# Layer norms between the stages of a two-layer decoder trunk: one GpSimd operation instead of four, residuals of the next weights behind the first modulated chunks, the accumulator filled later

## The chip, the core and the metric

The kernel runs on one core of one Trainium2 chip. The time is what the device measures for one execution, in microseconds (us). The kernel before has a median of 2310.28 us over three runs (2306.4, 2310.28 and 2311.95).

## The reference, cut to what matters

Two layers; each has a token mixer (forgetting attention in layer 0, sliding-window attention in layer 1) and then a gated ConvFFN. SEQ is 256, D_MODEL 2048, everything is float32.

```python
def layer_norm(x, g, b):
    mu = jnp.mean(xf, axis=-1, keepdims=True)
    var = jnp.mean(jnp.square(xf - mu), axis=-1, keepdims=True)
    y = (xf - mu) * lax.rsqrt(var + LN_EPS)
    return (y * g + b)
# every sub-layer:
# x <- LayerNorm(alpha * x + (1 + gate) * F(x * (1 + scale) + shift))
# shift, scale, gate: one vector of 2048 each, from the conditioning c times ada_w, plus ada_b
```

## The kernel before, in words

**Weights.** A float32 product is made of three reduced-precision ones. Each weight tile of 512 KB comes in by a DMA on the SP queue; ACT casts it to `wh` (L258); DVE takes the residual `wl = w - wh` (L269); PE multiplies the activations' halves `hH` and `hL` with `wh`, and `hH` with `wl`. There are four `wh`/`wl` buffers of each kind. `stream` makes one closure per tile, `go`, and puts it in the list `work`; `settle` calls the closures in turn, and `rest` emits the residuals of the tiles that stand next in `work`, across stage borders too: closures that are no tile (those added with `then`) are skipped and do not count.

**Borders.** Four sub-layers run one after the other, so there are three borders between stages and one end. Border 1 lies between layer 0's attention and its ConvFFN (about 492 to 507 us in the trace), border 2 between that and layer 1's attention (1258 to 1272), border 3 between layer 1's attention and its ConvFFN (1535 to 1555). At a border `residual` handles the last 512 columns for t = 0 and t = 1 (two halves of 128 rows each, called t0 and t1 below): DVE multiplies by the gate (L559, tile `t`), adds to `x` (L561), takes the statistics (L563, `stats`) and aggregates them (L566, `mv`: mean and variance). Then POOL (GpSimd) adds EPS (L568) and raises to -0.5 (L569), which gives `rs`; for t0 it also makes -mean * rs in two operations (L571, L572). `normalise` applies them 512 columns at a time: t0 on ACT (L582, from `rs` and the product), t1 on DVE (L584, from mean and `rs`). `between` calls `release` (below), `merged` (L616 to L618, vectors `G` and `B` on DVE) and `modulate`, which makes 8 chunks of two 128-column blocks each: PE transposes (L461), ACT writes `hH` (L471), DVE writes `t` and `hL` (L472, L473). Two chunks are made at once; the other six wait in the list `feeds`, and one follows each weight tile.

**The vectors from ada_w.** In the background `ada_vector` makes ten more vectors of shift, scale or gate: 32 tiles `wa` each, one DVE operation per tile into the accumulator `acc` (L384). `ada_tick` runs such a step whenever a rate that differs by stage has added up to one; `ada_need(l, v)` runs all steps still missing for a vector at the moment when it is wanted. At the end of a vector PE sums the partitions: 16 products with one column each (`sums`) and one small DVE operation for the result `cv` (L408). For the vectors in `HELD`, (0,4) and (1,4), which `between` needs at borders 1 and 3, the sums are put off to `release`. The vectors that follow them, (0,5) and (1,5), are gates, made with `row`: POOL clears `acc` first (L373, 128x2048) and a DMA on POOL's queue adds `ada_b` (L374). There is one buffer `acc`, so the clearing waits for the sums of the vector before.

Of the kernel before, what the change touches and what calls it, by code (L numbers as in the profile page):

```python
# [14 lines left out]
ALU = mybir.AluOpType  # L15
# [3 lines left out]
D = 2048  # L19
# [22 lines left out]
def hybrid_trunk(ctx: ExitStack, tc: tile.TileContext, a: dict, out: bass.AP):  # L42
# [34 lines left out]
    def pin(ins, on=True):  # L77

        if on:
            tc.keep_in_program_order(ins)  # L80
# [125 lines left out]

    feeds, post, work = [], [], []

    def then(fn):

        work.append(fn)
        if len(work) == 1 and not ahead[0]:
            settle()
# [9 lines left out]
    def rest(*items):  # L223

        n = 0
        for f in items:
            if f in residuals:
                residuals[f]()
                n += 1
            elif f in weights:  # L230
                n += 1
            if n > 2 - (items[0] not in weights):
                return

    residuals, weights = {}, set()

    def defer(gen):

# [11 lines left out]
    def stream(wsrc, row0, col, ks, use):  # L250

        for kc in ks[::2]:
            r0 = (row0 + kc) * P
            w = wtile()
            pin(nc.sync.dma_start(w, wsrc[r0:r0 + 2 * P, col:col + WB].rearrange("(k p) f -> p k f", p=P)), False)
            h = hl.tile([P, 2, WB], F32R, tag="wh", name="wh")
            l = hl.tile([P, 2, WB], F32R, tag="wl", name="wl")
            pin(nc.scalar.copy(h, w), False)  # L258

            def go(kc=kc, h=h, l=l):  # L260
                ahead[0] -= 1
                run_post()
                use(kc, h, l)
                if feeds:
                    feeds.pop(0)()
                tick()

            def residual_(w=w, h=h, l=l, go=go):
                pin(nc.vector.tensor_tensor(l, w, f32(h), op=ALU.subtract), False)  # L269
                del residuals[go]  # L270

            ahead[0] += 1
            weights.add(go)
            residuals[go] = residual_
            work.append(go)
            settle(2)
# [85 lines left out]
    def ada_vector(l, v):  # L362
        row = v % 3 == 2
        if (l, v) in HELD and HELD[l, v]:
            q = [cst.tile([P, 512], F32, tag=f"ha{i}", name="ha") for i in range(4)]
            part = lambda c, n: q[c // 512][:, c % 512:c % 512 + n]
            step_ = 512
        else:
            acc = cst.tile([P, D], F32, tag="acc", name="acc")
            part = lambda c, n: acc[:, c:c + n]  # L370
            step_ = D // 2
        if row:
            pin(nc.gpsimd.memset(acc, 0.0), True)  # L373
            nc.gpsimd.dma_start(acc[0:1, :], a["ada_b"][l:l + 1, v * D:(v + 1) * D])  # L374
        for k in range(KC):
            for c in range(0, D, D // 2):
                w = wtile("wa").rearrange("p a f -> p (a f)")
                pin(nc.sync.dma_start(w, a["ada_w"][l, k * P:(k + 1) * P, v * D + c:v * D + c + D // 2]), False)
                for o in range(0, D // 2, step_):
                    ac, wo = part(c + o, step_), w[:, o:o + step_]  # L380
                    if k == 0 and not row:
                        pin(nc.vector.tensor_scalar_mul(ac, wo, cact[:, 0:1]), True)
                    else:
                        pin(nc.vector.scalar_tensor_tensor(ac, wo, cact[:, k:k + 1], ac,  # L384
                                                           op0=ALU.mult, op1=ALU.add), True)
                yield
        if row:
            while not ada["gate_free"]:
                yield
            ada["gate_free"] = False  # L390
            g = cst.tile([P, D], F32, tag="gate", name="gate")
            for j in range(D // 512):
                ps = bank()
                mm(ps, ones, acc[:, j * 512:(j + 1) * 512], start=True, stop=True)
                yield
                nc.scalar.activation(g[:, j * 512:(j + 1) * 512], ps, AF.Copy, bias=1.0)
            gates[l, v] = g
            return
        ps = []

        def sums():
            ps.append(bank())
            for k in range(KC):
                pin(mm(ps[0][:, k:k + 1], part(k * P, P), ones[:, 0:1], start=True, stop=True))

        def finish():
            cv = cst.tile([P, KC], F32, tag=f"cv{v}", name="cv")
            pin(nc.vector.scalar_tensor_tensor(cv, ps[0][:, :KC], 1.0 if v % 3 else 0.0,  # L408
                                               acol[:, l, v * KC:(v + 1) * KC], op0=ALU.add, op1=ALU.add), True)
            cols[l, v] = cv  # L410

        if (l, v) in HELD:
            held.append((sums, finish))
            ada["held"] = not HELD[l, v]
            ready_cols.add((l, v))
        else:
            sums()
            yield
            finish()
# [136 lines left out]
    def residual(ps, d, gate, last):  # L556
        for t in range(NT):
            tmp = ttile()
            nc.vector.tensor_tensor(tmp, ps[t], gate[:, d * 512:(d + 1) * 512], op=ALU.mult)  # L559
            xs = x[:, t, d * 512:(d + 1) * 512]  # L560
            nc.vector.tensor_tensor(xs, xs, tmp, op=ALU.add)  # L561
            if last:
                nc.vector.bn_stats(stats[:, t, d, :], xs)  # L563
                if d == D // 512 - 1:
                    mv = sp.tile([P, 2], F32, tag="mv", name="mv")
                    nc.vector.bn_aggr(mv, stats[:, t].rearrange("p a b -> p (a b)"))  # L566
                    rs = sp.tile([P, 2], F32, tag="rs", name="rs")
                    nc.gpsimd.tensor_scalar_add(rs[:, 0:1], mv[:, 1:2], EPS)  # L568
                    nc.gpsimd.tensor_tensor(rs[:, 0:1], rs[:, 0:1], mhalf, op=ALU.pow)  # L569
                    if t == 0:  # L570
                        nc.gpsimd.tensor_tensor(rs[:, 1:2], rs[:, 0:1], mv[:, 0:1], op=ALU.mult)  # L571
                        nc.gpsimd.tensor_scalar_mul(rs[:, 1:2], rs[:, 1:2], -1.0)  # L572
                    moments[t] = (mv[:, 0:1], rs[:, 0:1], rs[:, 1:2])
            yield

# [96 lines left out]
    def out_proj(oT, full, w_o, l):  # L672
        def stat(kc, t):
            while kc not in full:
                step()
            return oT[kc][0][:, t * P:(t + 1) * P], oT[kc][1][:, t * P:(t + 1) * P]

        ps = {d: x_banks() for d in range(2)}

        def part(d, ks):  # L680
            use = x_mm_end(ps[d], stat, KC, 2) if d == D // WB - 1 else                 lambda kc, h, l_: x_mm(ps[d], kc, h, l_, stat, KC - 1)
            stream(w_o, 0, d * WB, ks, use)

        for i, ks in enumerate((range(0, 8), range(8, 12))):
            then(lambda i=i: ada.update(rate=((1.4,1.4,1.8,1.8), (0.9,)*4)[l][i]))
            for d in range(2):
                part(d, list(ks))
        then(lambda: ada_need(l, 2))
        for d in range(D // WB):
            if d < 2:  # L690
                part(d, list(range(12, KC)))
            else:
                then(lambda d=d: ada.update(rate=((1.4,1.4,1.8,1.8), (0.9,)*4)[l][d]))
                ps[d] = x_banks()
                part(d, list(range(KC)))
            then(lambda d=d: defer(residual(ps[d], d, gates[l, 2], True)))
        then(lambda: (flush(), ada.update(gate_free=True)))


    def fox(l, j):  # L700
# [277 lines left out]
    def conv_ffn(l):  # L978
# [37 lines left out]
        for si, (b0, b1) in enumerate(sbs):  # L1016
# [20 lines left out]
            then(ready)  # L1037
            for d in range(D // WB):
                ps = x_stationary(w_dn, d * WB, b0 * 4, (b1 - b0) * 4, stat, (2, 4)[l] if si > 0 and d == D // WB - 1 else 0)
                then(lambda ps=ps, d=d, si=si: defer(residual(ps, d, gates[l, 5], si == len(sbs) - 1)))  # L1040
        then(lambda: (flush(), ada.update(gate_free=True)))


    def between(l, v, g, b, name, ll):

        ada_need(l, v)
        ada_need(l, v + 1)
        release()
        modulate(*merged(l, v, g, b, ll), normalise)
        later([affine(name, ll)])  # L1050

    for l in range(DEPTH):
        if l > 0:
            then(lambda l=l: (between(l, 0, 2, 3, "ln_ffn", l - 1), ada.update(rate=.3)))
            swa(l, l // 2)
        else:
            fox(l, l // 2)
        then(lambda l=l: between(l, 3, 0, 1, "ln_mix", l))
        conv_ffn(l)
    settle()  # L1060
    gb, bb = ln_rows("ln_ffn", DEPTH - 1)
# [34 lines left out]
```

## Time and profile before

| what | value |
|---|---|
| median of the three runs | 2310.28 us (2306.4 to 2311.95) |
| the profiled execution's own time | 2307.69 us |
| its span in the trace | 2305.9 us |
| PE busy (matmul) | 2232.5 us, 97% of the span |
| PE weight load busy | 2047.7 us, 89% |
| DVE busy | 1803.7 us, 78% |
| ACT busy | 1137.8 us, 49% |
| POOL busy | 40.1 us, 2% |
| mean granted TensorE clock | 0.986 of full speed |

The span is the part of the execution that the profiler sees on the core; 1.8 us lie around it. PE is busy nearly all the time, so time can be lost or won where PE waits. POOL is hardly used; what matters there is who waits for it. In the timelines below "start us, us" is the start of a row and how long it ran, `x4` says that four like instructions stand in one row, and the bracket at the end gives the engine's idle time before the row and what ended it.

### The profile page before, as it was taken

How to read it: one execution, taken by the hardware profiler on the slowest of the kernel's cores; microseconds unless marked ns; L12 is line 12 of the kernel's file. 1: busy time of each engine (PE TensorE's matmuls, PEld its weight loads, DVE VectorE, ACT ScalarE, POOL GpSimd, SP SyncE). 2: the span in 40 equal slices, each digit the busy share in tenths (PEclk: the TensorE clock that was granted, in tenths of full speed). 3: DMA queues.
4: the chain of work that ended last, by engine and by line, in shares of the span. 5: the costliest groups of instructions: out<-in, count | busy, mean ns of one | idle time of the engine just before them, and what ended most of it. 6: DMA issues, size and time to landing. Idle time of an engine off the chain costs nothing.

```text
span 2305.9 us, 38661 instructions
## 1 busy us (share of the span) xinstructions
PE 2232.5 (97%) x15061; PEld 2047.7 (89%) x15061; DVE 1803.7 (78%) x2609; ACT 1137.8 (49%) x1685; POOL 40.1 (2%) x79
## 2 busy tenths in 40 slices
PE   5899999899999999999999999999999999999997
PEld 5799988789999988999987778779999988999986
DVE  7888978979977876887886998899878655666656
ACT  1336653545555533454543578745555533455532
POOL 1001000010000000000001000000000000000000
PEclk9999999999999999999999999999999999999999
DMA  9998989969887897887887685788888566666663
GB/s 322 329 351 269 350 321 352 327 212 312 302 263 243 291 312 257 292 285 257 274 299 255 212 302 182 236 291 276 265 265 256 180 193 193 191 188 188 190 191 112
DMA packets 285561, 598.86 MB, mean 260 GB/s; under 512 B 20790, under 2 KB 53816, under 8 KB 285376
## 3 DMA queue, kind: packets, MB, share of 16 engines
q1 hardware_dynamic: 284768, 595.85, 78.4%
q8 instruction: 118, 1.93, 0.3%
q0 software_dynamic: 608, 0.53, 0.1%
q14 instruction: 67, 0.55, 0.1%
HBM read 594.21 MB, written 2.10 MB: 259 GB/s over the span
## 4 chain that ended last, share of the span: by engine, by line
PE 87%; DVE 8%; ACT 3%; issue 2%; POOL 0%; DMA 0%; SPq 0%; DVEq 0%; ACTq 0%; POOLq 0%
PE ws L75 51%; PE xs L75 31%; DVE wl L269 2%; DVE acc L384 2%; PE sm L75 1%; PE cps L75 1%; ACT wh L258 1%; PE S L75 1%; PE o L75 1%; DVE oacc L516 1%; PE sm L461 1%; ACT pr L635 0%; ACT pr L643 0%; PE T L655 0%; DVE x L561 0%
## 5 line engine op out<-in xcount | busy, mean ns | idle before, releaser
L269 DVE TENSOR_TENSOR wl<-w,wh 128x1024 fp32r<-128x1024 f32 x728 | 888.9, 1222 | 397.2 <-ACT wh L258 369.8
L258 ACT CAST wh<-w 128x1024 fp32r<-128x1024 f32 x728 | 764.2, 1052 | 861.5 <-PE ws L75 320.0
L75 PE MATMUL ws<-hH,wh 128*128 128x256 f32 x3328 | 938.9, 282 | 6.0 <-ACT wh L258 6.0
L75 PE MATMUL ws<-hH,wl 128*128 128x256 f32 x3328 | 930.6, 281 | 4.0 <-DVE wl L269 3.9
L75 PE MATMUL ws<-hL,wh 128*128 128x256 f32 x3328 | 931.6, 280 | 0.2 <-DVE hL L85 0.2
L75 PEld LDWEIGHTS ws<-hH,wh 128*128 128x128 f32 x3328 | 629.4, 189 | 10.0 <-ACT wh L258 6.8
L75 PEld LDWEIGHTS ws<-hH,wl 128*128 128x128 f32 x3328 | 627.7, 189 | 5.6 <-DVE wl L269 5.5
L75 PEld LDWEIGHTS ws<-hL,wh 128*128 128x128 f32 x3328 | 629.2, 189 | 2.7 <-issue 1.9
L75 PE MATMUL xs<-wh,gT 128*128 128x512 f32 x1408 | 438.1, 392 | 0.0
L384 DVE SCALAR_TENSOR_TENSOR acc<-wa,cact,acc 128x1024 f32<-128x1024 f32 x308 | 391.8, 1278 | 0.0
L75 PEld LDWEIGHTS xs<-wh,gT 128*128 128x128 f32 x1408 | 266.5, 189 | 55.9
L75 PE MATMUL xs<-wl,gT 128*128 128x512 f32 x704 | 275.7, 392 | 0.0
L75 PEld LDWEIGHTS xs<-wl,gT 128*128 128x128 f32 x704 | 133.3, 189 | 27.3
L75 PE MATMUL xs<-wl,hH 128*128 128x512 f32 x352 | 141.0, 401 | 5.1 <-DVE wl L269 5.1
L75 PE MATMUL xs<-wh,hL 128*128 128x512 f32 x352 | 139.9, 399 | 0.4 <-DVE hL L85 0.4
L75 PE MATMUL xs<-wh,hH 128*128 128x512 f32 x352 | 139.6, 406 | 0.2 <-ACT hH L471 0.2
L75 PE MATMUL xs<-wh,oT 128*128 128x512 f32 x384 | 125.5, 397 | 1.0 <-ACT pT L657 0.9
L985 ACT ACTIVATE u<-ws,ccol 128x256 f32<-128x256 f32 x176 | 96.7, 562 | 58.5 <-PE ws L75 51.3
L986 DVE SCALAR_TENSOR_TENSOR u<-ws,ccol,u 128x255 f32<-128x255 f32 x176 | 82.5, 478 | 20.0 <-ACT u L985 20.0
L75 PEld LDWEIGHTS xs<-wh,oT 128*128 128x128 f32 x384 | 72.6, 190 | 16.1 <-ACT pT L657 1.3
L75 PEld LDWEIGHTS xs<-wl,hH 128*128 128x128 f32 x352 | 66.5, 189 | 22.1 <-DVE wl L269 8.0
L988 DVE SCALAR_TENSOR_TENSOR u<-ws,ccol,u 128x254 f32<-128x254 f32 x176 | 83.4, 478 | 2.0
(211 smaller groups left out, 1559.6 us busy)
## 6 DMA issues: line engine op xcount, KB each, us to landing
w<-in_ffn_w_up_dram SPq DMA_DIRECT2D x352, 512.0 KB, 4.6
wa<-in_ada_w_dram SPq DMA_DIRECT2D x320, 512.0 KB, 5.2
w<-in_ffn_w_down_dram SPq DMA_DIRECT2D x176, 512.0 KB, 5.0
w<-in_fox_w_in_dram SPq DMA_DIRECT2D x96, 512.0 KB, 5.9
wo<-in_ada_w_dram SPq DMA_DIRECT2D x64, 512.0 KB, 7.7
w<-in_swa_w_in_dram SPq DMA_DIRECT2D x40, 512.0 KB, 4.7
w<-in_fox_w_o_dram SPq DMA_DIRECT2D x32, 512.0 KB, 6.8
w<-in_swa_w_o_dram SPq DMA_DIRECT2D x32, 512.0 KB, 5.7
```

Source lines behind the costliest of these rows:

```text
L75: return nc.tensor.matmul(o, lhsT, rhs, start=start, stop=stop, **kw)
L258: pin(nc.scalar.copy(h, w), False)
L269: pin(nc.vector.tensor_tensor(l, w, f32(h), op=ALU.subtract), False)
L384: pin(nc.vector.scalar_tensor_tensor(ac, wo, cact[:, k:k + 1], ac, op0=ALU.mult, op1=ALU.add), True)
L461: nc.tensor.transpose(o[:, t * P:(t + 1) * P], x[:, t, (k + j) * P:(k + j + 1) * P], ident)
L516: nc.vector.scalar_tensor_tensor(acc[:, v, k % 2, :], w[:, k, :], cact[:, kc:kc + 1], acc[:, v, k % 2, :], op0=ALU.mult, op1=ALU.add)
L985: nc.scalar.activation(u, pf, AF.Identity, bias=cw(CW, f), scale=cw(2, f))
L986: nc.vector.scalar_tensor_tensor(u[:, 1:], pf[:, :S - 1], cw(1, f), u[:, 1:], op0=ALU.mult, op1=ALU.add)
L988: nc.vector.scalar_tensor_tensor(u[:, 2:], pf[:, :S - 2], cw(0, f), u[:, 2:], op0=ALU.mult, op1=ALU.add)
```

## The change

It has three parts. (1) In the layer norm EPS is added on DVE, onto the variance in `mv` (new L577); POOL keeps only the power (new L578); for t0 the product -mean * rs is made by one DVE operation (new L580). (2) `rest` stops at a closure that is marked `alone`: the closures at the borders are marked, and while the first two chunks are made no residual of the second and later tiles of the next stage is emitted; the two that come next are pinned behind them (`behind`). (3) A gate vector that follows a held one, (0,5) or (1,5), runs four empty steps before it clears `acc`.

```diff
+    def then(fn, alone=False):
+        if alone:
+            lone.add(fn)
...
         for f in items:
+            if f in lone:
+                n = max(n, 2)
             if f in residuals:
                 residuals[f]()
                 n += 1
...
             def residual_(w=w, h=h, l=l, go=go):
-                pin(nc.vector.tensor_tensor(l, w, f32(h), op=ALU.subtract), False)
+                pin(nc.vector.tensor_tensor(l, w, f32(h), op=ALU.subtract), behind[0] > 0)
+                behind[0] -= 1
                 del residuals[go]
...
         if row:
+            if (l, v - 1) in HELD:
+
+                for _ in range(4):
+                    yield
             pin(nc.gpsimd.memset(acc, 0.0), True)
...
-                    nc.gpsimd.tensor_scalar_add(rs[:, 0:1], mv[:, 1:2], EPS)
-                    nc.gpsimd.tensor_tensor(rs[:, 0:1], rs[:, 0:1], mhalf, op=ALU.pow)
+                    nc.vector.tensor_scalar_add(mv[:, 1:2], mv[:, 1:2], EPS)
+                    nc.gpsimd.tensor_tensor(rs[:, 0:1], mv[:, 1:2], mhalf, op=ALU.pow)
                     if t == 0:
-                        nc.gpsimd.tensor_tensor(rs[:, 1:2], rs[:, 0:1], mv[:, 0:1], op=ALU.mult)
-                        nc.gpsimd.tensor_scalar_mul(rs[:, 1:2], rs[:, 1:2], -1.0)
+                        nc.vector.scalar_tensor_tensor(rs[:, 1:2], mv[:, 0:1], -1.0, rs[:, 0:1],
+                                                       op0=ALU.mult, op1=ALU.mult)
...
-            then(lambda d=d: defer(residual(ps[d], d, gates[l, 2], True)))
-        then(lambda: (flush(), ada.update(gate_free=True)))
+            then(lambda d=d: defer(residual(ps[d], d, gates[l, 2], True)), d == D // WB - 1)
+        then(lambda: (flush(), ada.update(gate_free=True)), True)
...
         modulate(*merged(l, v, g, b, ll), normalise)
+        behind[0] = 2
         later([affine(name, ll)])
```

The last `residual` of layer 1's ConvFFN passes and the calls of `between` get the same mark. Lines of the new kernel have new numbers: L269 is L273 there, L384 is L393, L408 L417, L472 and L473 L481 and L482, L559 to L566 are L568 to L575, L584 L593, L616 to L618 L625 to L627, and the clearing L373 is L382.

How instructions move on DVE at border 1, before, from the aggregation of t0 to the first normalised columns of t1 (`wl` is the residual of a tile of the next stage, `cv` the result of the held vector (0,4)):

```order
L566 BN_AGGR mv<-stats 128x2
L269 TENSOR_TENSOR wl<-w,wh 128x1024
L559 TENSOR_TENSOR t<-xs,gate 128x512
L269 TENSOR_TENSOR wl<-w,wh 128x1024
L561 TENSOR_TENSOR x<-x,t 128x512
L563 BN_STATS stats<-x 128x6
L566 BN_AGGR mv<-stats 128x2
L408 SCALAR_TENSOR_TENSOR cv<-sm,acol 128x16
L616 TENSOR_TENSOR G<-cv,lcol 128x16
L617 TENSOR_TENSOR B<-cv,lcol 128x16
L584 TENSOR_SCALAR x<-x,mv,rs 128x512
```

and the same stretch of DVE in the new kernel:

```order
L575 BN_AGGR mv<-stats 128x2
L577 TENSOR_SCALAR mv<-mv 128x1
L580 SCALAR_TENSOR_TENSOR rs<-mv,rs 128x1
L568 TENSOR_TENSOR t<-xs,gate 128x512
L570 TENSOR_TENSOR x<-x,t 128x512
L572 BN_STATS stats<-x 128x6
L575 BN_AGGR mv<-stats 128x2
L577 TENSOR_SCALAR mv<-mv 128x1
L417 SCALAR_TENSOR_TENSOR cv<-sm,acol 128x16
L593 TENSOR_SCALAR x<-x,mv,rs 128x512
L625 TENSOR_TENSOR G<-cv,lcol 128x16
L626 TENSOR_TENSOR B<-cv,lcol 128x16
```

The two residuals between t0 and t1 are gone (a third, further up, too; they stand behind the two chunks now), t0's product L580 stands between t0 and t1, and G and B stand behind the first normalised columns.

POOL's operations around borders 1 and 2, before (the first clearing is that of gate (0,5), the second that of a later gate):

```order
L568 TENSOR_SCALAR rs<-mv 128x1
L569 TENSOR_TENSOR rs<-rs,mhalf 128x1
L571 TENSOR_TENSOR rs<-rs,mv 128x1
L572 TENSOR_SCALAR rs<-rs 128x1
L568 TENSOR_SCALAR rs<-mv 128x1
L569 TENSOR_TENSOR rs<-rs,mhalf 128x1
L373 MEMSET acc 128x2048
L374 DMA acc<-in_ada_b_dram 1x16x128
```

and in the new kernel, from the powers of border 1 to those of border 2:

```order
L578 TENSOR_TENSOR rs<-mv,mhalf 128x1 x2
L382 MEMSET acc 128x2048
L383 DMA acc<-in_ada_b_dram 1x16x128
L382 MEMSET acc 128x2048
L383 DMA acc<-in_ada_b_dram 1x16x128
L578 TENSOR_TENSOR rs<-mv,mhalf 128x1 x2
```

Three operations for t0 and one for t1 have left POOL; the clearing still stands directly behind the power of t1, and what it waits for is the same last product of the sums as before.

DVE at border 3, before (`acc` rows are steps of the held vector (1,4)), from the last of its steps to the aggregation of t0:

```order
L384 SCALAR_TENSOR_TENSOR acc<-wa,cact,acc 128x1024 x2
L269 TENSOR_TENSOR wl<-w,wh 128x1024 x2
L384 SCALAR_TENSOR_TENSOR acc<-wa,cact,acc 128x1024
L269 TENSOR_TENSOR wl<-w,wh 128x1024 x3
L559 TENSOR_TENSOR t<-xs,gate 128x512
L561 TENSOR_TENSOR x<-x,t 128x512
L563 BN_STATS stats<-x 128x6
L269 TENSOR_TENSOR wl<-w,wh 128x1024
L566 BN_AGGR mv<-stats 128x2
```

and in the new kernel, from the second last residual before the border to the first normalised columns of t1:

```order
L273 TENSOR_TENSOR wl<-w,wh 128x1024
L393 SCALAR_TENSOR_TENSOR acc<-wa,cact,acc 128x1024
L273 TENSOR_TENSOR wl<-w,wh 128x1024
L393 SCALAR_TENSOR_TENSOR acc<-wa,cact,acc 128x1024 x2
L568 TENSOR_TENSOR t<-xs,gate 128x512 x2
L570 TENSOR_TENSOR x<-x,t 128x512 x2
L572 BN_STATS stats<-x 128x6 x2
L575 BN_AGGR mv<-stats 128x2 x2
L577 TENSOR_SCALAR mv<-mv 128x1 x2
L393 SCALAR_TENSOR_TENSOR acc<-wa,cact,acc 128x1024
L580 SCALAR_TENSOR_TENSOR rs<-mv,rs 128x1
L593 TENSOR_SCALAR x<-x,mv,rs 128x512
```

The four empty steps after (0,4) push all later vectors back: `ada_need` has two steps of (1,4) left to run at border 3 where there was none, three `acc` steps more stand ahead of t0, and the last one stands behind the aggregations of both halves.

More of the change, by code (lines that the diff above doesn't have):

```diff
@@ L207, in hybrid_trunk @@
     feeds, post, work = [], [], []
-    def then(fn):
+    def then(fn, alone=False):
+        if alone:
+            lone.add(fn)
         work.append(fn)
@@ L233, in rest @@
                 return
-    residuals, weights = {}, set()
+    residuals, weights, lone, behind = {}, set(), set(), [0]
     def defer(gen):
@@ L1039, in conv_ffn @@
                 ps = x_stationary(w_dn, d * WB, b0 * 4, (b1 - b0) * 4, stat, (2, 4)[l] if si > 0 and d == D // WB - 1 else 0)
-                then(lambda ps=ps, d=d, si=si: defer(residual(ps, d, gates[l, 5], si == len(sbs) - 1)))
-        then(lambda: (flush(), ada.update(gate_free=True)))
+                then(lambda ps=ps, d=d, si=si: defer(residual(ps, d, gates[l, 5], si == len(sbs) - 1)),
+                     si > 0 and d == D // WB - 1)
+        then(lambda: (flush(), ada.update(gate_free=True)), True)
     def between(l, v, g, b, name, ll):
@@ L1053, in hybrid_trunk @@
         if l > 0:
-            then(lambda l=l: (between(l, 0, 2, 3, "ln_ffn", l - 1), ada.update(rate=.3)))
+            then(lambda l=l: (between(l, 0, 2, 3, "ln_ffn", l - 1), ada.update(rate=.3)), True)
             swa(l, l // 2)
@@ L1057, in hybrid_trunk @@
             fox(l, l // 2)
-        then(lambda l=l: between(l, 3, 0, 1, "ln_mix", l))
+        then(lambda l=l: between(l, 3, 0, 1, "ln_mix", l), True)
         conv_ffn(l)
```

## The prediction

> **What bounds the kernel now.** I read the page's busy shares first, then PE's own waits, then the timelines of the three borders and of the end, last the granted clock there. The page's first part and three rows of PE's waits (engine, line, releaser: us in total, times, longest):
>
> ```profile
> PE 2232.5 (97%) x15061; PEld 2047.7 (89%) x15061; DVE 1803.7 (78%) x2609; ACT 1137.8 (49%) x1685; POOL 40.1 (2%) x79
> PE xs L75 <- DVE wl L269: 11.7, 11, 2.3
> PE sm L461 <- ACT x L582: 6.7, 3, 5.0
> PE sm L461 <- DVE x L584: 4.4, 2, 2.4
> ```
>
> PE bounds the kernel. The change touches its waits for normalised `x`, 11.1 us in 5 places, and the thin work around them (sums, transposes); 0.3% of the time, about what a measurement of this kernel can tell from no change, is 6.9 us, so nearly all of those waits would have to go. Border 1, on DVE, POOL and PE (start, length):
>
> ```profile
> 495.11 0.26 DVE L566 BATCH_NORM_AGGREGATE mv<-stats 128x2 f32<-128x24 f32 x1
> 495.41 1.22 DVE L269 TENSOR_TENSOR wl<-w,wh 128x1024 fp32r<-128x1024 f32 x1
> 496.55 0.68 DVE L559 TENSOR_TENSOR t<-xs,gate 128x512 f32<-128x512 f32 x1
> 497.15 1.21 DVE L269 TENSOR_TENSOR wl<-w,wh 128x1024 fp32r<-128x1024 f32 x1
> 498.29 0.68 DVE L561 TENSOR_TENSOR x<-x,t 128x512 f32<-128x512 f32 x1
> 499.00 0.69 DVE L563 BATCH_NORM_STATS2 stats<-x 128x6 f32<-128x512 f32 x1
> 499.73 0.26 DVE L566 BATCH_NORM_AGGREGATE mv<-stats 128x2 f32<-128x24 f32 x1
> 499.91 0.11 DVE L408 SCALAR_TENSOR_TENSOR cv<-sm,acol 128x16 f32<-128x16 f32 x1
> 501.01 2.00 DVE L584 TENSOR_SCALAR x<-x,mv,rs 128x512 f32<-128x512 f32 x1 [0.69 <-POOL rs L569]
> 503.01 0.99 DVE L584 TENSOR_SCALAR x<-x,mv,rs 128x512 f32<-128x512 f32 x2
> 495.46 1.26 POOL L568 TENSOR_SCALAR rs<-mv 128x1 f32<-128x1 f32 x1 [289.49 <-DVE mv L566]
> 498.50 0.56 POOL L572 TENSOR_SCALAR rs<-rs 128x1 f32<-128x1 f32 x1
> 500.40 0.58 POOL L569 TENSOR_TENSOR rs<-rs,mhalf 128x1 f32<-128x1 f32 x1
> 500.92 1.80 POOL L373 MEMSET acc<- 128x2048 f32 x1
> 495.52 3.63 PE L75 MATMUL sm<-ones,acc 128*128 128x1 f32 x32
> 499.96 1.11 PE L461 MATMUL sm<-ident,x 128*128 128x128 f32 x4 [0.81 <-ACT x L582]
> 503.06 1.11 PE L461 MATMUL sm<-ident,x 128*128 128x128 f32 x4 [1.99 <-DVE x L584]
> 504.19 0.80 PE L75 MATMUL ws<-hH,wh 128*128 128x256 f32 x2
> ```
>
> POOL's four operations for t0 run from 495.46 to 499.06, but the wait that ends last is t1's: aggregation at 499.99, power at 500.98, and then a normalisation of 2.00 us that runs beside the clearing, where two later ones take 0.99 together. The next two borders, 2 first (DVE, PE), then 3:
>
> ```profile
> 1257.04 1.28 DVE L384 SCALAR_TENSOR_TENSOR acc<-wa,cact,acc 128x1024 f32<-128x1024 f32 x1
> 1260.29 0.67 DVE L559 TENSOR_TENSOR t<-xs,gate 128x512 f32<-128x512 f32 x1
> 1265.83 1.46 DVE L584 TENSOR_SCALAR x<-x,mv,rs 128x512 f32<-128x512 f32 x3 [0.98 <-POOL rs L569]
> 1270.26 0.75 DVE L473 TENSOR_TENSOR hL<-t,hH 128x256 fp32r<-128x256 f32 x2
> 1275.11 0.69 DVE L85 TENSOR_TENSOR hL<-t,hH 128x512 fp32r<-128x512 f32 x1
> 1265.22 2.32 PE L461 MATMUL sm<-ident,x 128*128 128x128 f32 x8 [5.01 <-ACT x L582]
> 1267.80 0.79 PE L75 MATMUL xs<-wh,hH 128*128 128x512 f32 x1 [0.25 <-ACT hH L471]
> 1524.00:1536.00 12.00, 11.98 (x53) 9.58 (x53) 12.00 (x14) 5.03 (x5) 0.00 (x0) 1.00 1.05 393
> 1535.20 1.27 DVE L384 SCALAR_TENSOR_TENSOR acc<-wa,cact,acc 128x1024 f32<-128x1024 f32 x1
> 1539.80 0.67 DVE L559 TENSOR_TENSOR t<-xs,gate 128x512 f32<-128x512 f32 x1
> 1547.78 2.00 DVE L584 TENSOR_SCALAR x<-x,mv,rs 128x512 f32<-128x512 f32 x1 [0.68 <-POOL rs L569]
> 1542.20 3.63 PE L75 MATMUL sm<-ones,acc 128*128 128x1 f32 x32
> 1549.84 1.12 PE L461 MATMUL sm<-ident,x 128*128 128x128 f32 x4 [2.44 <-DVE x L584]
> 1550.97 0.80 PE L75 MATMUL ws<-hH,wh 128*128 128x256 f32 x2
> ```
>
> In the stretch row (PE, PEld, DVE, ACT, POOL busy, then the clock) DVE is busy for all 12 us: ahead of border 3 DVE has no slack. Last the clock; the columns are the same:
>
> ```profile
> 499.60:506.00 6.40, 4.04 (x16) 3.24 (x17) 5.47 (x14) 4.85 (x9) 3.18 (x4) 0.50 0.22 88
> 1264.20:1270.60 6.40, 5.04 (x18) 3.75 (x18) 4.90 (x13) 5.01 (x9) 0.90 (x3) 0.50 0.39 129
> 1547.40:1553.80 6.40, 3.95 (x17) 3.55 (x18) 5.84 (x12) 4.42 (x8) 2.73 (x3) 0.50 0.14 48
> ```
>
> After each border PE resumes at half clock. So work begun earlier, in the half-clock stretch, yields only half of its lead, if that stretch ends where it ends now; if it ends earlier by the same lead, all of it. [...]
>
> **The change, border 1.** By the order nothing ahead of it moves but one residual. t0's aggregation ends at 495.37. The added EPS and the product L580 are as small as `cv`, 0.11 each; the power is 0.58. With a handover of 0.05 on either side L580 ends at 496.3: the new wait of DVE for POOL is about 0.75, and t1's chain stands behind it. It replaces two residuals, 1.1 each as they overlap. t1 then takes 0.72 a step (499.73 − 499.00): aggregated at 498.75, EPS 498.9, power at 499.5. The sums end at 499.15, so the clearing becomes free to start with that power's end, as it is today, and meets the same normalisation: 2.00 us, to about 501.5 against 503.01. That the accumulator is filled later is not so here, by the order. G and B stand behind the first normalised columns, and the sum for B behind the second (0.5): 502.3, where ACT can begin `hH` 1.27 earlier than now. Half of that lies in the half clock: **−0.65** (−1.3 if the clock follows; −2.8 if the clearing keeps out of the way, 1.5 more). [...]
>
> The residuals of tiles 1 to 3 now stand behind the chunks. PE takes 0.226 us a product in the full stretch above (53 in 11.98), so 2.7 for a tile's 12 of 512 columns (24 of 256 here); estimated from that, tile 1's residual is ready some 1 us ahead of it, and the parts of `hL` that follow about 0.5 us ahead. This cover is thin: what is lost beyond it would be lost outright.
>
> **Border 2** has no sums and no clearing. t1's gated product at 1260.29 waits for PE's last product, before and after, and L580 is done by then. From 1260.29: three steps of 0.72, aggregation 0.26, EPS, handovers, power 0.58: 1263.6 instead of 1265.83, a lead of 2.2. With half the lead kept: −1.1. If the clock follows, the residuals may decide: two chunks end at 1268.8, then two residuals (1.14 each), a chunk's `t`, a third residual, and `hL` at about 1273.4, which today is there at 1275.80, while PE's need for it comes forward to about 1272.2 (resumption at 1265.6, two tiles of 2.7, and 1.2 of transposes): 1.2 of the lead is lost, 1.0 left. **−1.1** (−2.2 with neither, +1.3 if the three residuals, 3.5 us, delay PE wholly).
>
> **Border 3.** Today the last `acc` step is done at 1536.47, well ahead of the sums at 1542.20. By the order the four empty steps put three of these steps in front of t0's chain, and the last one behind both aggregations; one residual less stands ahead. On a full DVE t0's start moves from 1539.80 to between that and 1542.4 (3 × 1.2 − 1.1 later). t1's product is anyway not ready before PE's end of the stage, about 1542.4 (the sums start at 1542.20). From there t1's product, two sums into `x`, two statistics (0.6 to 0.7 each), two aggregations, EPS twice, and the step of 1.27: it ends between 1547.5 and 1548.2; I take 1547.7. The second half of the sums (16 of 32, 1.8 us) waits for it: 1549.5. Then `cv`; the clearing starts as well and meets the second normalised columns, behind which G and B stand: 1551.6; the rest of B and the third columns, `hH` at 1552.5, first `ws` at 1553.1 instead of 1550.97: +2.1. [...]
>
> **End.** The last norm's DVE wait for POOL:
>
> ```profile
> 2290.50 1.44 DVE L1068 SCALAR_TENSOR_TENSOR x<-x,rs,ln 128x512 f32<-128x512 f32 x2 [0.47 <-POOL rs L569]
> ```
>
> With one operation fewer ahead of it 0.47 goes, 0.1 of EPS comes: **−0.4**. The many other steps moved between borders (background `acc` in the ConvFFN stages) lie beside a PE that is fed anyway: nothing, up to what a full DVE costs, in the rival below.
>
> **Sum:** −0.65 − 1.1 + 2.75 − 0.4 = +0.6 on the profiled 2307.69, which is 2308.3. That execution stood 2.6 under the median of 2310.28; on the median it is 2310.9.
>
> **The rivals.**
> *A. Faster, by over 6.9.* [...] Chance 0.2. [...]
> *B. Slower: DVE bounds the sliding-window stage.* At both of its ends DVE gets work that it did not have: 3 residuals (3.5 us) behind border 2's chunks and 3 `acc` steps (3.6 us) before border 3, where it is full. It decides where those steps stand ahead of residuals that PE needs next; PE already waits 11.7 us for `wl`. Uncovered: −0.65 + 1.3 + 2.75 + 3.6 − 0.4 = +6.6, and with border 1's residuals late by 0.65 too +7.3: 2317.6. Against it: PE loses only 0.02 in the full stretch, so it is fed with some lead. Chance 0.2.
> *C. The forecast,* with the parts cancelling: 0.6, by its own bounds 2303.6 (−2.8 − 2.2 − 1.3 − 0.4 = −6.7) to 2313.3 (−0.65 + 1.3 + 2.75 − 0.4 = +3.0).
>
> **How the numbers follow.** 2311 is C's. For 8 in 10 the range reaches from A's better half, 2301, to B's, 2318. Faster by over 0.3% (under 2303.4) takes A, 0.2; slower (over 2317.2) takes most of B, 0.18; the rest is no difference, 0.62.
>
> **What would show it.** In the new profile: the power of t0 about 0.58 and DVE's wait for it 0.75 at border 1; a normalisation of 2.0 beside the clearing there; border 2's first normalised columns 2.2 after the same PE end earlier; and at border 3 an `acc` step (new L393) behind the two aggregations, with sums in two parts and PE's wait for `x` longer than 2.44. I am wrong if the clearing starts behind the first chunk, if that `acc` step ends before 1546, or if PE's waits for `wl` grow by more than 3 us.

## The result, and the profile after

Over 13 runs each on the same chips the changed kernel has a median of 2316.51 us (2310.25 to 2319.07) and the kernel before 2309.80 us (2304.75 to 2314.95). The ratio is 1.0023, 95% interval 1.0014 to 1.0031: slower by some 5 us. The ratio lies inside the 0.3% that the prediction called no difference (its interval reaches just past that), and the median inside the range of 2301 to 2318, but near the upper end and far from the +0.6 us of the sum. The profiled execution took 2310.95 us (span 2309.2), 3.3 over the one shown of before. It is the second shortest of the 13, and the two medians lie 6.7 us apart: what follows accounts for the 3.3 us between the profiles, and where the other runs lose more is not shown.

The page's busy shares and PE's waits after the change:

```profile
PE 2236.5 (97%) x15061; PEld 2051.6 (89%) x15061; DVE 1804.1 (78%) x2621; ACT 1136.7 (49%) x1685; POOL 31.8 (1%) x63
```

```profile
PE xs L75 <- DVE wl L273: 12.1, 11, 2.3
PE sm L470 <- DVE x L593: 4.1, 2, 2.1
PE sm L75 <- DVE acc L393: 3.3, 1, 3.3
PE sm L470 <- ACT x L591: 1.9, 1, 1.9
```

The wait of the transposes for `x` fell from 11.1 us to 6.0, and a wait of the sums for an `acc` step, 3.3 us, is new. Border 1 (DVE, POOL, PE):

```profile
496.06 0.16 DVE L580 SCALAR_TENSOR_TENSOR rs<-mv,rs 128x1 f32<-128x1 f32 x1 [0.68 <-POOL rs L578]
498.31 0.26 DVE L575 BATCH_NORM_AGGREGATE mv<-stats 128x2 f32<-128x24 f32 x1
499.44 2.00 DVE L593 TENSOR_SCALAR x<-x,mv,rs 128x512 f32<-128x512 f32 x1 [0.25 <-POOL rs L578]
499.35 1.80 POOL L382 MEMSET acc<- 128x2048 f32 x1
502.85 0.79 PE L75 MATMUL ws<-hH,wh 128*128 128x256 f32 x2 [0.25 <-ACT hH L480]
```

DVE waits 0.68 for the power of t0, t1 is aggregated 1.42 earlier than before, and the first normalisation still runs 2.00 us beside the clearing. Border 2 (DVE, PE):

```profile
1258.36 0.69 DVE L568 TENSOR_TENSOR t<-xs,gate 128x512 f32<-128x512 f32 x1 [0.74 <-PE xs L75]
1261.68 0.16 DVE L580 SCALAR_TENSOR_TENSOR rs<-mv,rs 128x1 f32<-128x1 f32 x1 [0.68 <-POOL rs L578]
1265.04 1.91 DVE L593 TENSOR_SCALAR x<-x,mv,rs 128x512 f32<-128x512 f32 x4 [0.66 <-POOL rs L578]
1266.77 0.80 PE L75 MATMUL xs<-wh,hH 128*128 128x512 f32 x1
```

Border 3 (DVE, POOL, ACT, PE):

```profile
1546.08 1.29 DVE L393 SCALAR_TENSOR_TENSOR acc<-wa,cact,acc 128x1024 f32<-128x1024 f32 x1
1551.13 2.02 DVE L593 TENSOR_SCALAR x<-x,mv,rs 128x512 f32<-128x512 f32 x1
1551.06 1.80 POOL L382 MEMSET acc<- 128x2048 f32 x1 [3.28 <-PE sm L75]
1553.95 1.93 ACT L480 ACTIVATE hH<-sm,B,G 128x256 fp32r<-128x256 f32 x4 [4.24 <-DVE B L627]
1547.43 3.57 PE L75 MATMUL sm<-ones,acc 128*128 128x1 f32 x16 [3.35 <-DVE acc L393]
1554.56 0.79 PE L75 MATMUL ws<-hH,wh 128*128 128x256 f32 x2 [1.75 <-ACT hH L480]
```

The last `acc` step stands behind the aggregations; the second half of the sums follows it and takes 3.57 us for 16 products, where before 32 took 3.63; then `cv`, the clearing beside a normalisation, and the sum for B, for which ACT waits 4.24 us. The granted clock is 0.50 in these 3.57 us; read in stretches of 0.2 us, it is 0.50 from 1547.37 to 1557.61, before from 1547.30 to 1554.12.

A measure for the experiments is the stretch from the end of PE's last large product before a border to the start of the first of the next stage, read from PE's timeline. It is 8.51, 7.58 and 8.62 us before and 7.34, 5.72 and 12.45 after.

Two profiles that can be set against each other start to end are this one and a second one of the kernel before (the run `e10_before_again` below), since the half clock lies at the same place in both (at border 2 from 1264.07 to 1270.90 us in this one, from 1264.09 to 1270.92 in the other). Where the 3.3 us between them arise, by PE's large products and the casts of weight tiles:

| stretch | change, us |
|---|---|
| up to border 1 | −0.1 |
| border 1 (24th product of the stage after it) | −0.6 |
| layer 0's ConvFFN | +1.45 |
| border 2 | −0.5 |
| layer 1's attention | −0.5 |
| border 3 | +3.75 |
| layer 1's ConvFFN and the end | −0.2 |

The +1.45 is not at a border. In that stage PE makes the sums of three background vectors; the row of the first sums, and the clock (last but two) in the 10 us stretches around and behind them, first before:

```profile
869.96 3.63 PE L75 MATMUL sm<-ones,acc 128*128 128x1 f32 x32
```

```profile
870.00:880.00 10.00, 10.00 (x55) 8.69 (x54) 2.49 (x4) 2.09 (x2) 0.00 (x0) 0.83 0.38 121
880.00:890.00 10.00, 10.00 (x46) 8.29 (x45) 8.56 (x11) 4.22 (x4) 0.00 (x0) 1.00 0.73 228
```

and the same two views after:

```profile
885.66 4.13 PE L75 MATMUL sm<-ones,acc 128*128 128x1 f32 x32
```

```profile
880.00:890.00 10.00, 10.00 (x59) 9.02 (x58) 5.77 (x7) 3.15 (x3) 0.00 (x0) 0.93 0.82 267
890.00:900.00 10.00, 10.00 (x34) 7.90 (x34) 2.00 (x3) 2.10 (x2) 0.00 (x0) 0.73 0.27 82
```

PE is busy throughout, yet it falls to half clock behind the sums: for (1 − 0.83) × 10 / 0.5 = 3.4 us before and for (0.07 + 0.27) × 10 / 0.5 = 6.8 us after. Read in stretches of 0.2 us, the clock is 0.50 from 874.87 to 878.28 before and from 888.60 to 895.43 after. All half-clock stretches of these two traces but the last, which reaches the end, are 3.41, 6.83 or 10.24 us long: one, two or three windows, as 3.41 us are called here. Before, the half clock starts 1.28 us behind the end of the row, after, 2.94 us behind its start. One window more costs 1.7 us, by estimate: half of 3.41. A row as long is not always followed by half clock. In the same stage of the profile of before:

```profile
1050.36 3.63 PE L75 MATMUL sm<-ones,acc 128*128 128x1 f32 x32
1050.00:1060.00 10.00, 10.00 (x89) 10.00 (x88) 6.23 (x12) 4.45 (x8) 0.00 (x0) 1.00 0.39 114
```

Here the clock stays at 1.00. Nor does an extra window need the empty steps: of the kernels below without them, `e3_norm_only` and `e7_no_clear` have two windows behind the first row (6.83 us from 880.63, 6.8 us between 875 and 885), `e5_product_later` none; `e6_faster_rate`, with the steps, has two (6.8 us between 885 and 895). So the +1.45 is what these two executions show. It is not shown that the change costs this in each execution.

### The profile page after: what moved, and what is told of

Same layout as the page of the kernel before. It is cut to its first block, busy times and chain, and to the rows that moved or that the text cites. A ratio compares the mean times of both kernels' runs of the same rounds, so it can differ in the third digit from the quotient of the medians.

```text
span 2309.2 us, 38649 instructions
## 1 busy us (share of the span) xinstructions
PE 2236.5 (97%) x15061; PEld 2051.6 (89%) x15061; DVE 1804.1 (78%) x2621; ACT 1136.7 (49%) x1685; POOL 31.8 (1%) x63
## 4 chain that ended last, share of the span: by engine, by line
PE 84%; DVE 9%; ACT 3%; issue 2%; DMA 1%; POOL 0%; SPq 0%; DVEq 0%; ACTq 0%; POOLq 0%
PE ws L75 50%; PE xs L75 29%; DVE wl L273 2%; DVE acc L393 2%; PE sm L75 1%; PE cps L75 1%; ACT wh L262 1%; DVE oacc L525 1%; PE S L75 1%; PE o L75 1%; PE sm L470 1%; ACT pr L644 0%; ACT pr L652 0%; DMA wa<-in_ada_w_dram 0%; DVE pr L640 0%
## 5 line engine op out<-in xcount | busy, mean ns | idle before, releaser
L273 DVE TENSOR_TENSOR wl<-w,wh 128x1024 fp32r<-128x1024 f32 x728 | 888.9, 1222 | 397.8 <-ACT wh L262 368.9
L393 DVE SCALAR_TENSOR_TENSOR acc<-wa,cact,acc 128x1024 f32<-128x1024 f32 x308 | 391.7, 1278 | 0.0
```

## The experiments

**Each part by itself.** The first theory was that the loss comes from the empty steps, at border 3; the second, that it comes from the residuals behind the chunks.

`e1_no_steps`, the changed kernel without part 3:

```diff
-            if (l, v - 1) in HELD:
-                for _ in range(4):
-                    yield
```

> Parts 1 and 2 of the change without the four empty steps. First theory (the loss stands at border 3 and comes from the empty steps, which put acc steps into that border): PE gains about 0.5 us at border 1, 0.5 to 1 at border 2 and 0.5 to 1 at border 3, nothing at the end, so 1.5 to 2.5 us faster than before, ratio about 0.999; PE resumes at border 3 earlier than before, no acc step stands behind the aggregations. Second theory (the residuals put behind the chunks cost, on a DVE that is full): still slower than before, by 2 us or more, ratio 1.001 or above.

Measured: 2310.87 us against 2312.69, ratio 0.9994 (0.9984 to 1.0004). Stretches 7.33, 5.72, 7.31. At border 3 (PE):

```profile
1542.37 3.62 PE L75 MATMUL sm<-ones,acc 128*128 128x1 f32 x32
1549.83 0.80 PE L75 MATMUL ws<-hH,wh 128*128 128x256 f32 x2 [0.24 <-ACT hH L476]
```

The sums are in one piece again, and border 3 is 1.3 us shorter than before instead of 3.8 longer. The time is not distinguished from before; the second theory's 1.001 lies outside the interval.

`e2_steps_only`, the kernel before with these three lines added at the same place:

> The kernel before with the four empty steps and nothing else. First theory: the whole loss is here, borders 1 and 2 as before, border 3 about 3.5 to 4.5 us longer than before, ratio 1.0015 to 1.003, with sums of (1,4) in two parts. Second theory: no difference from before, ratio 0.999 to 1.001.

Measured: 2322.05 us, ratio 1.0046 (1.0034 to 1.0058); stretches 8.51, 7.58 and 17.72. DVE, then PE, at border 3:

```profile
1553.07 1.22 DVE L388 SCALAR_TENSOR_TENSOR acc<-wa,cact,acc 128x1024 f32<-128x1024 f32 x1
1557.13 3.41 PE L75 MATMUL sm<-ones,acc 128*128 128x1 f32 x16
1564.78 0.80 PE L75 MATMUL ws<-hH,wh 128*128 128x256 f32 x2 [3.28 <-ACT hH L475]
```

The sign and the place are as the first theory says; the size, 9.1 us more at border 3, is over twice what was expected. Here the second half of the sums stands on PE behind t0's transposes, and these wait for POOL's four operations and ACT:

```profile
1556.22 1.11 PE L465 MATMUL sm<-ident,x 128*128 128x128 f32 x4 [6.06 <-ACT x L586]
```

So the sums start 2.84 us after the last `acc` step ends, not at once as with all three parts.

`e3_norm_only`, the kernel before with the diff of the layer norm alone:

> The kernel before with part 1 alone: EPS and the product on DVE. Both theories: the four POOL operations of t0 become one, but t1's chain on DVE bounds the border and keeps its residuals, so the resumption of PE moves by under 0.5 us at borders 1 and 3; at border 2, where t0's operations on POOL ended late (first transposed x waits 5.0 us for ACT), up to 1.5 us earlier. Together 0 to 2 us faster, ratio 0.999 to 1.000.

Measured: 2317.30 us, ratio 1.0020 (1.0010 to 1.0030); stretches 9.26, 7.90, 9.35, each longer than before by 0.3 to 0.75. The expectation was wrong in sign. At border 1 (DVE, POOL):

```profile
502.91 0.16 DVE L571 SCALAR_TENSOR_TENSOR rs<-mv,rs 128x1 f32<-128x1 f32 x1 [0.46 <-POOL rs L569]
501.38 1.49 POOL L569 TENSOR_TENSOR rs<-mv,mhalf 128x1 f32<-128x1 f32 x1 [289.68 <-DVE mv L568]
```

The power takes 1.49 us beside a residual on DVE (501.22, 1.23 us long), and t0's product waits for it, with t1's whole chain queued behind on DVE. The power of t1 in the prediction's rows takes 0.58 where no residual runs. At the borders before, DVE waited for none of t0's operations on POOL. Not all of the time is the border's. By PE's large products, as in the table above, its profile loses 5.9 us ahead of 125 us (the opening, below) and 1.6 behind the sums in layer 0's ConvFFN; border 1 takes 1.9, border 2 nothing and border 3 0.3.

`e4_behind_only`, part 2 alone (the changed kernel without part 3 and with the five old lines of the layer norm):

> The kernel before with part 2 alone: residuals behind the first two chunks, POOL keeps its four operations. [...] Second theory: slower by 1 us or more, with PE's waits for wl longer by as much.

Measured: 2311.16 us, ratio 0.9998 (0.9988 to 1.0008), where the first theory had 0.999 to 1.000; stretches 6.80, 5.30, 6.80. At border 1 (DVE):

```profile
501.32 0.26 DVE L571 BATCH_NORM_AGGREGATE mv<-stats 128x2 f32<-128x24 f32 x1
502.97 1.72 DVE L589 TENSOR_SCALAR x<-x,mv,rs 128x512 f32<-128x512 f32 x1
```

The stretches are the shortest of the four: POOL's four operations, no longer beside residuals, take 1.8 us there (498.86 to 500.64), 3.6 before, and are done before t1 needs POOL at 501.67. Part 1 on top of part 2 costs 0.4 to 0.5 us a border. Yet 1.7 to 2.3 us less at each border shows in no time that can be told from before: in its profile 0.2 is kept at border 1, 0.2 at border 2 and 1.3 at border 3, and ahead of border 1 PE already stands 3.4 later (its sums there start at 498.92, before at 495.52).

**Causes taken away.** `e5_product_later`: as `e1_no_steps`, and t0's product is pinned behind t1's gated product and sum, which are pinned too:

```diff
...
+            if behind_t:     # last columns, t == 1
+                mu_, rs_, nm_ = moments[0]
+                pin(nc.vector.scalar_tensor_tensor(nm_, mu_, -1.0, rs_, op0=ALU.mult, op1=ALU.mult))
```

> Parts 1 and 2 without the empty steps, with t0's product -mean*rs on DVE placed behind t1's gated product and sum instead of ahead of them. With parts 1 and 2 the stretch from PE's last product to the first of the next stage was 7.33, 5.72 and 7.31 us at the three borders, with part 2 alone 6.80, 5.30 and 6.80: part 1 costs 0.4 to 0.5. Theory: that is t1's chain on DVE queued behind the product, which waits 0.7 us for POOL; then these stretches become about 6.6, 5.0 and 6.6, shorter than with part 2 alone. Rival: it is EPS on DVE and the place of G and B behind the first normalised columns; then they stay at 7.3, 5.7 and 7.3.

Measured: 2310.10 us against 2312.48, ratio 0.9988 (0.9975 to 1.0000); stretches 7.03, 5.06, 7.03. DVE at border 1:

```profile
496.94 0.15 DVE L570 SCALAR_TENSOR_TENSOR rs<-mv,rs 128x1 f32<-128x1 f32 x1
499.08 0.17 DVE L413 SCALAR_TENSOR_TENSOR cv<-sm,acol 128x16 f32<-128x16 f32 x1 [0.84 <-PE sm L75]
499.17 2.02 DVE L590 TENSOR_SCALAR x<-x,mv,rs 128x512 f32<-128x512 f32 x1
```

The product no longer waits. Border 2 gains 0.66, about what was expected. At borders 1 and 3 it is only 0.3, and the stretches stay longer than with part 2 alone, against the expectation: `cv` now waits 0.84 for the sums, and the normalisation behind it runs beside the clearing. The time can't be told from `e1_no_steps` (0.9994).

`e6_faster_rate`, the changed kernel with faster background steps in layer 1's attention:

```diff
-            then(lambda i=i: ada.update(rate=((1.4,1.4,1.8,1.8), (0.9,)*4)[l][i]))
+            then(lambda i=i: ada.update(rate=((1.4,1.4,1.8,1.8), (1.15,)*4)[l][i]))
...
```

The same stands in the output projection.

> The changed kernel with the rate of background steps in the two projections of layer 1's attention at 1.15 instead of 0.9 (in the input and output projections), so that (1,4) is whole before border 3 in spite of the empty steps. Theory (the late acc step is the whole loss at border 3): the stretch there falls from 12.45 us to about 7.3, as without the empty steps, and the time to the level of e1_no_steps, ratio 0.999 to 1.000. Rival (the empty steps cost through a fuller DVE in the attention stage): the stretch falls, but PE's waits for wl grow by about as much, and the time stays over 1.001.

Measured: 2313.87 us, ratio 1.0003 (0.9992 to 1.0015); border 3's stretch 7.58 instead of 12.45. PE's waits for residuals:

```profile
PE xs L75 <- DVE wl L273: 14.8, 12, 2.3
PE ws L75 <- DVE wl L273: 2.0, 2, 1.3
```

16.8 us in all, 15.6 before. With the empty steps kept and the last `acc` step in time the loss at border 3 is gone: that step was its cause. The rival's fuller DVE shows too: in layer 1's attention, about 1510 us, PE waits 1.71 and 1.11 us for `wl` where after the change it waits 0.56 once.

`e7_no_clear`, `e1_no_steps` without clearing for (0,5) and (1,5): their first step multiplies into `acc`, and `ada_b` is added from a tile of its own (`fresh` is true for these two):

```diff
...
-                    if k == 0 and not row:
+                    if k == 0 and not (row and not fresh):
...
+                if row and fresh and k == 8:
+                    wb = wtile("wb").rearrange("p a f -> p (a f)")
+                    nc.sync.dma_start(wb[0:1, :], a["ada_b"][l:l + 1, v * D + c:v * D + c + D // 2])
+                    yield
+                    pin(nc.vector.tensor_tensor(acc[0:1, c:c + D // 2], acc[0:1, c:c + D // 2], wb[0:1, :], op=ALU.add), True)
```

> Parts 1 and 2 without the empty steps, and no clearing at borders 1 and 3: for (0,5) and (1,5) the first step writes the accumulator with a plain multiplication, and ada_b is added later by DVE from a tile of its own. Theory (the clearing doubles more than the length of the first normalisation): the first normalisation takes 0.55 us instead of 2.00, and the stretch at borders 1 and 3 shrinks from 7.3 to about 6.0; 5.72 at border 2 stays. Rival: the sums or the sum for B end last there; then the stretch shrinks by under 0.5.

Measured: 2310.08 us, ratio 0.9990 (0.9981 to 1.0000); stretches 5.89, 5.73, 5.88. DVE at border 1:

```profile
504.08 0.55 DVE L597 TENSOR_SCALAR x<-x,mv,rs 128x512 f32<-128x512 f32 x1 [0.24 <-POOL rs L582]
```

0.55 instead of 2.00, and 1.4 us less in the stretch at both borders. This is what "the accumulator filled later" would have been worth there; in the time it can't be told from `e1_no_steps`.

`e8_spread_sums`, the kernel before with the background sums in pieces (a piece takes no step from the rate, and a tick makes at most two steps):

```diff
...
+            for k in range(KC):
+                pin(mm(ps[0][:, k:k + 1], part(k * P, P), ones[:, 0:1], start=True, stop=True))
+                if k % 4 == 3 and k < KC - 1:
+                    yield "free"
...
```

> The kernel before with the sums of the four vectors that are not held issued in four pieces of four columns, one piece per weight tile, instead of 16 columns in a row. In the traces so far PE runs at half clock for one or two windows of 3.4 us behind such a row of sums in a ConvFFN stage (about 875 and 1225 us), though it is never idle there. [...] Rival: it isn't the sums (the clock drops there for another reason): no difference.

Measured: 2307.80 us, ratio 0.9980 (0.9967 to 0.9992), within the 0.997 to 0.999 that were expected if the row of sums brings the half clock. The clock around the same sums:

```profile
870.00:880.00 10.00, 10.00 (x58) 8.62 (x57) 3.94 (x4) 3.14 (x3) 0.00 (x0) 1.00 0.57 178
1225.00:1235.00 10.00, 10.00 (x56) 8.57 (x56) 6.81 (x9) 3.00 (x3) 1.81 (x1) 1.00 0.48 153
```

The half clock is gone at both places (1.00 in these rows; before, 0.83 from 870 to 880 and 0.66 from 1225 to 1235), and no piece in this profile or the next run's is followed by any: the rows in one piece were its cause. It wins 5.3 us in layer 0's ConvFFN against the second profile of before. But the half-clock stretches at borders 2 and 3 are three windows long here instead of two (10.24 us for 6.83), and 1.4 of the 5.3 are lost again there.

**Together.** `e9_together` has parts 1 and 2, the product later, no clearing at the borders, and the sums in pieces:

> What the runs point to, put together: parts 1 and 2 without the empty steps, t0's product behind t1's gated product and sum, no clearing at borders 1 and 3, the other sums in pieces. Stretches from PE's last product to the first of the next stage: without the clearing and with the earlier aggregation of t1 about 5.4 to 5.9 at borders 1 and 3 (the end of the sums plus cv and the normalisation, 3.6 + 1.9, bounds them), 5.06 at border 2; no half clock at 875 and 1225. If the gains add (0.2 to 0.3% from the sums, 0.1% each from the others): ratio 0.995 to 0.997. If the clock's windows take back what an earlier start gives: 0.997 to 0.998, no better than e8_spread_sums.

Measured: 2295.99 us against 2311.11, ratio 0.9942 (0.9928 to 0.9955), better than expected and the shortest of all. Stretches 5.56, 5.06, 5.64. Border 3 (DVE, PE), then the clock at borders 2 and 3:

```profile
1537.28 0.54 DVE L607 TENSOR_SCALAR x<-x,mv,rs 128x512 f32<-128x512 f32 x1
1539.24 0.80 PE L75 MATMUL ws<-hH,wh 128*128 128x256 f32 x2 [0.25 <-ACT hH L493]
```

```profile
1257.20:1260.20 3.00, 2.98 (x9) 2.09 (x10) 3.00 (x8) 2.58 (x5) 0.00 (x0) 0.50 0.03 5
1260.60:1263.00 2.40, 2.40 (x15) 2.03 (x13) 2.40 (x5) 1.02 (x2) 0.00 (x0) 1.00 0.00 0
1537.00:1540.20 3.20, 2.95 (x13) 2.38 (x14) 3.01 (x10) 2.67 (x6) 0.00 (x0) 0.50 0.00 0
1540.40:1543.60 3.20, 3.20 (x17) 3.20 (x16) 3.20 (x7) 1.23 (x3) 0.00 (x0) 0.50 0.00 0
```

The ratios of the single runs add up to about 0.996. Against the third profile of before, whose windows lie at the same place, PE's products come 1.4 us earlier by border 1, another 5.3 in layer 0's ConvFFN, 1.6 at border 2 and 2.6 at border 3. The half-clock stretch is one window at border 2, two as before at border 3, where `e8_spread_sums` alone had three at each. So the shorter stretches are kept in good part here; one profile does not show that another place would keep as much.

**The windows.** In every trace all edges of the half clock lie at one place in a period of 3.413 us, the length of the shortest half-clock stretches (in `e1_no_steps`, `e2_steps_only` and `e4_behind_only` read from where the spacing of PE's products at the borders changes, in the others from the clock): at 1.05 in the profile of before, 1.13 after, but 2.26 in `e2_steps_only` and 3.41 in `e3_norm_only`. Three further profiles asked whether the program sets it.

> The kernel before, once more, for a second profile. In the traces so far the half-clock stretches of one execution all begin and end at one and the same place in a period of 3.413 us, and this place differs from kernel to kernel, also in the opening (up to 125 us), which is the same work in all of them. Theory: the windows run free of the program, so the same kernel has another place in another execution, and with it another number of half-clock stretches in the opening (3 at places 0.9 to 1.6 us, 5 at 2.1 to 3.4), worth up to 6 us. Rival: the place belongs to the program; then it is 1.05 us again and the opening has the same three stretches.

> The kernel before a third time, for a third profile; as for e10_before_again: another place in the period by the theory, the same place 1.05 us by the rival.

> Part 1 alone once more, for a second profile of that kernel. Three profiles of the kernel before have their half-clock edges at 1.05, 1.15 and 0.85 us of the 3.413 us period, the first of this one has them at 3.41. If the place belongs to the program, it is near 3.4 again, with five half-clock stretches in the opening and a time near 2317; if the windows run free of it, another place, and with one from 0.9 to 1.6 three stretches and a time about 5 us shorter.

Measured: 1.15 and 0.85 for the kernel before (2307.67 and 2307.35 us), 2.42 for part 1 alone (2316.42 us). Clock in two stretches of the opening, the second profile of before, then the second of part 1 alone:

```profile
60.00:90.00 30.00, 24.29 (x153) 21.95 (x151) 25.37 (x56) 9.01 (x12) 0.00 (x0) 0.89 1.05 347
90.00:120.00 30.00, 28.22 (x204) 25.92 (x203) 24.56 (x50) 11.65 (x15) 0.00 (x0) 1.00 0.95 313
```

```profile
60.00:90.00 30.00, 26.02 (x140) 23.03 (x139) 22.20 (x51) 8.15 (x10) 0.00 (x0) 0.77 0.96 316
90.00:120.00 30.00, 28.29 (x191) 26.63 (x190) 24.43 (x51) 12.49 (x16) 0.00 (x0) 0.89 0.94 301
```

The work in these 60 us is the same, the half clock is not: 6.6 us of it in two stretches against 20.4 in five, and by 125 us the same products of PE come 4.8 us later in `e2_steps_only`, 5.9 in `e3_norm_only` and 4.9 in the second profile of part 1 alone than in the second profile of before: that much of their profiles' time comes from the opening, which the edits don't touch. One kernel had two places (3.41 and 2.42), so the program alone does not set it; but the kernel before had nearly the same place three times, and what does set it stays open. The stretches at the borders did not change with it: part 1 alone gave 9.27, 7.90 and 9.35 the second time.

## Why the prediction was right, and where its steps were not

The time fell into the range, and at borders 1 and 3 the mechanism is the predicted one. Two of its terms were off in the same direction, so that the range was needed.

- *Border 1.* An `hH` 1.27 earlier was predicted, and −0.65 kept. PE's first product came 1.17 earlier relative to its last one, −0.6 was kept, and the clearing met the normalisation as the order had it. DVE's wait was 0.68 (0.75 predicted). Right in each step.
- *Border 2.* The lead of the first normalised columns was to be 2.2 and was 1.6, that of PE's first product 1.86. The step that failed is "t1's gated product at 1260.29 waits for PE's last product ... and L580 is done by then". From t0's gated product to L580 it takes 3.3 us (1258.36 to 1261.68 after), and PE's last product ended at 1261.05: t1 stood 0.6 behind it. The row of before that starts t0's chain (below) already says so, since 3.3 us on from it is past 1260.29. −0.5 was kept at the border, and another 0.5 appears by the end of the stage, together near the −1.1; the way of the second half was not followed, so this agreement may be luck.

```profile
1258.24 0.68 DVE L559 TENSOR_TENSOR t<-xs,gate 128x512 f32<-128x512 f32 x1
```

- *Border 3.* The mechanism was right: three steps ahead of t0, the last behind both aggregations (it ended at 1547.37; 1547.7 was taken), sums in two parts. The term that was mis-sized is the second half of the sums, "16 of 32, 1.8 us": 3.57, at a granted clock of 0.50. PE resumed at 1554.56 instead of 1553.1, and +3.75 stood in the place of +2.75. No run shows the +2.75 of the sum, nor a PE that resumes at 1553.1; in their place the half clock lasted 10.24 us with the resumption at 1554.56, and 6.83 before. The −1.3 of the bounds for this border is what the stretch of `e1_no_steps` shows (8.62 to 7.31). One sign did not come either: PE's wait for `x` was not longer than 2.44 there; PE waited 3.35 for the `acc` step and 1.75 for `hH` instead.
- *End.* −0.4 was predicted. t0's first row there to the end of DVE's last takes 0.1 longer than before: the product on DVE waits 0.46 for POOL, as the normalisation had (0.47), and two small operations came on top:

```profile
2293.03 0.16 DVE L580 SCALAR_TENSOR_TENSOR rs<-mv,rs 128x1 f32<-128x1 f32 x1 [0.46 <-POOL rs L578]
```

- *"A PE that is fed anyway: nothing".* This missed the +1.45 of the sums in layer 0's ConvFFN: PE is fed, but behind a row of one-column products its clock fell to 0.50 for 3.4 us before and 6.8 after.
- *Rivals.* Of B's price the residuals behind the chunks are refuted: part 2 alone is not slower, and PE's waits for `wl` grew by 0.4 us (12.1 for 11.7), not by more than 3. The three `acc` steps ahead of border 3 did cost, but through the last of them and not through late residuals. No run shows the 2301 that the range takes from A: with the change the half clock lasted 6.83 us at borders 1 and 2, as before, and 3.41 longer at border 3. What the clearing out of the way gives at a border, `e7_no_clear` shows: 1.4 us. `e9_together` gains 15.1 us, more than A's 6.9, but without the empty steps and with the sums in pieces.

The forecast of no difference rested on −1.75 − 0.4 against +2.75. The two profiles put +3.75 and +1.45 against about −1.9, which is 3.3 and not 0.6; the width of the range covered the rest.

## What to carry to other kernels

An idle step in a paced background queue is not free: it delays everything behind it, up to the next point where something must be whole; look there, not where the step stands. Moving a small operation from an idle engine to one on whose queue the critical chain stands can lose time even if it makes the operation count smaller (part 1 on top of part 2: 0.4 to 0.5 us a border); put the one that waits behind the work that doesn't. And rows of one-column products are worth breaking up among large ones: that alone gave 0.2% here (0.08 to 0.33%), where no part of the change gave a gain that can be told from nothing.

## What the runs showed of the hardware

- The TensorE clock fell to half behind about 3.6 us of one-column products although PE was busy all the time (clock 0.83 in 10 us before, 0.73 after), and did not when they came in pieces of a quarter (1.00 in `e8_spread_sums`). Not every row in one piece did it: behind the one at 1050 us before, the clock stayed at 1.00.
- All half-clock edges of an execution share one place in a period of 3.413 us, and the half clock came and went in stretches of 3.41, 6.83 or 10.24 us. Each 3.41 us of it costs a PE that is busy in them 1.7, by estimate from products of 512 columns that start 0.43 us apart at half clock and 0.23 at full (border 2 before, 1268.81 to 1271.48). The place changed between the two profiles of part 1 alone (3.41, 2.42) and hardly among three of before (0.85 to 1.15).
- The opening alone has 6.6 or 20.4 us of half clock between 60 and 120 us by that place. The spread of some 11 us among runs of one kernel goes with the clock: of the 29 runs of the kernel before beside `e1_no_steps` to `e4_behind_only`, the 8 with a mean granted clock of 0.986 or more took 2304.66 to 2309.59 us, the other 21 2310.80 to 2315.75. Whether it is the opening in those runs, no profile shows.
